# A hybrid encoder layer on one core: gates moved into a three-stage seven-product tail, divisions and roots on GpSimd, and every engine's order written by a list scheduler

## The chip, the core and the metric

The kernel runs on one core of one Trainium2 chip. The metric is device time in microseconds, the median of several executions. The engines are called TensorE (PE; PEld are its weight loads), VectorE (DVE), ScalarE (ACT), GpSimd (POOL) and SyncE (SP, whose queue issues the DMAs).

## What is computed

One layer, applied to two requests of 2048 tokens with 1024 features each, all in float32:

```python
h = rms_norm(x, norm_w)
q_a, k_a, v_a, g_a, q_b, k_b, v_b, g_b = split(h @ w_in)      # 512 128 128 512 512 512 512 512 columns
o_a = windowed_gqa_sink(rope(rms(q_a)), rope(rms(k_a)), v_a, sink) * silu(g_a)   # 8 heads, 2 key heads, +-128 tokens
o_b = neighbourhood_attn(rms(q_b), rms(k_b), v_b, rpb) * silu(g_b)               # 8 heads, 64-wide grid, window 8 x 16
x = x + concat(o_a, o_b) @ w_out
y = x + (p @ w_ple) * sigmoid(x @ w_ple_gate)
```

Both softmaxes are full ones (maximum, exponential, sum, division); group A has one more term, the sink, in its sum.

## The kernel before, in words

**Precision.** A float32 operand is split into a high part (`fp32r`) and the rest, and a product is made of three matmuls: high-high, high-low, low-high. So each 128-row step of a projection is three matmuls, and a 1024-row projection is 24 of them. A split is a ScalarE copy (high) and a subtraction (low) on VectorE or GpSimd.

**Stages.** Tokens go in tiles of 128, 16 a request. Group A has 32 tiles (`f` below 32), group B 64: two halves of four heads, each 32 tiles (8 rows x 16 columns of the grid).

- *Projections* are made by generators. `proj_a(f)` makes `pk` (keys and values, 256 columns, 24 matmuls), `pq` (queries, 512 columns, 24) and `pg` (gate A, 512 columns, 24). `proj_b(f)` makes `pqk` (512 columns) and `pvg` (values and gate, 512 columns). After the matmuls come the squares, `rsqrt` (a bit trick and three Newton steps, 11 small VectorE instructions), the normalisation, for A the rotation on GpSimd, for the gates `tanh` and one VectorE product into `gs`.
- *Attention* is made of units: `unit_a(f, kv)`, two a tile, and `unit_b(f)`, one a tile, four heads each. `sc` makes scores; `softmax` adds mask or bias and takes the maximum (VectorE, L204); `exps` does the exponential (L219) and reciprocal, and multiplies reciprocal and gate on GpSimd into `g` (L229). The probabilities are not divided. `pt` transposes them through TensorE and splits them, `po` multiplies by values, `fin` transposes the gate `g` (`pgt`, `pgtb`), multiplies it with the output (L539, L697) and stores it to `oa_d` or `ob_d` in HBM. `prep_a`/`prep_b` transpose queries and `split_q` splits them; L240 is the ScalarE copy that shifts a high half to the other 64 partitions.
- *Tail.* 16 output tiles of 256 tokens. Four are made directly (`out_ahead`, `pout`, 192 matmuls of 256 columns each) while the last units run. The other twelve go through six groups of 512 tokens in which a 2 x 2 block product is made of seven block products instead of eight (`STEPS`, `prep`, `product`, `result`); then eight such groups make the second stage, the sigmoid gate of the embedding. A block product is 48 matmuls of 256 columns (L973). `prep` makes sums of blocks (L939 to L950) and splits them; `result` adds the pieces. In the second stage `ple_of` makes the embedding product (`pple`) between the block products. The sums of weight blocks are made by GpSimd during group B (`combine`) and kept in `sums`. Between the two stages each weight quarter is replaced as soon as the last group has used it.

**Order.** `mm` and `tr` pin TensorE's order to program order (`pinned`). Units are interleaved with projections by hand: `PLAN_A` and `PLAN_B` say at which share of a unit's time each part is issued, and `stream` yields projection matmuls with their costs (215 for 512 columns) in between. Other engines follow the order in which the program names their instructions. All loads and stores are issued by SP, in order.

**Buffers.** PSUM: three banks for projections, three for scores and transposes, two for the rest (`PSB`). Five score buffers `s` in SBUF (`SB`), three `p_t`, five for V windows.

Of the kernel before, what the change touches and what calls it, by code (L numbers as in the profile page):

```python
# [46 lines left out]
def bias_offsets():  # L47
# [25 lines left out]
PLAN_A = (
# [3 lines left out]
)  # L77
PLAN_B = (
    (0.00, 1, "sc", 0), (0.03, 1, "sc", 1), (0.07, 1, "sc", 2), (0.09, 0, "po", 2), (0.11, 1, "sc", 3), (0.16, 0, "po", 3),
    (0.24, 0, "fin", 0), (0.35, 1, "prep", 0),  # L80
    (0.45, 1, "pt", 0), (0.52, 1, "pt", 1), (0.60, 1, "pt", 2), (0.66, 1, "po", 0), (0.74, 1, "pt", 3), (0.80, 1, "po", 1),
)


def emit(ctx, tc, io):
# [3 lines left out]
    pp = ctx.enter_context(tc.tile_pool(name="psum", bufs=2, space=bass.MemoryType.PSUM))  # L89

    def ptile(shape, tag, name):
        tag = PSM.get(tag, tag)
        return pp.tile(shape, F32, tag=tag, name=name, bufs=PSB[tag])

    ident = cp.tile([128, 128], F32, tag="ident", name="ident")
    make_identity(nc, ident)
    nw = cp.tile([128, KT], F32, tag="nw", name="nw")
    nc.sync.dma_start(nw, io["norm_w"])
    ms_a = cp.tile([128, 2 * NT], F32, tag="ms_a", name="ms_a")
    rs_b = cp.tile([128, 2 * NT], F32, tag="rs_b", name="rs_b")  # L100
    hr_b = cp.tile([128, 2 * NT], F32, tag="hr_b", name="hr_b")
    ep_b = cp.tile([128, 2 * NT], F32, tag="ep_b", name="ep_b")
    ms_b = cp.tile([128, 2 * NT], F32, tag="ms_b", name="ms_b")
    wk = cp.tile([128, 2], F32, tag="wk", name="wk")
    wkt = cp.tile([128, 4], F32, tag="wkt", name="wkt")
    nc.sync.dma_start(wkt, io["qk_norms"])
    nc.vector.tensor_tensor(out=wk[:, 0:1], in0=wkt[:, 0:1], in1=wkt[:, 1:2], op=ALU.mult)
    nc.vector.tensor_tensor(out=wk[:, 1:2], in0=wkt[:, 2:3], in1=wkt[:, 3:4], op=ALU.mult)
    nc.vector.tensor_scalar_mul(wk, wk, 0.125)
    nc.vector.memset(wk[0:16, 0:1], 0.125)  # L110
    nc.vector.memset(wk[64:80, 0:1], 0.125)
# [5 lines left out]

    def rsqrt(pool, v, y, n, tag):
        i2 = pool.tile([128, n], I32, tag=tag + "i", name=tag + "i")
        a = pool.tile([128, n], F32, tag=tag + "a", name=tag + "a")  # L120
        nc.vector.tensor_scalar(out=i2, in0=v.bitcast(I32), scalar1=1, scalar2=None,
                                op0=ALU.logical_shift_right)
        nc.vector.tensor_scalar(out=y.bitcast(I32), in0=i2, scalar1=-1, scalar2=0x5F3759DF,
                                op0=ALU.mult, op1=ALU.add)
        for _ in range(3):
            nc.vector.scalar_tensor_tensor(out=a, in0=y, scalar=-0.5, in1=y, op0=ALU.mult, op1=ALU.mult)
            nc.vector.tensor_tensor(out=a, in0=a, in1=v, op=ALU.mult)
            nc.vector.scalar_tensor_tensor(out=y, in0=a, scalar=1.5, in1=y, op0=ALU.add, op1=ALU.mult)

    copies = []  # L130

    def copied(src, rows, width):

        n = src.shape[1]
        d = dram.tile([rows, n], F32, tag=src.tensor.name + "_c", name=src.tensor.name + "_c")
        copies.extend((d[128 * j:128 * j + 128, c:c + width], src[128 * j:128 * j + 128, c:c + width])
                      for c in range(0, n, width) for j in range(rows // 128))
        return d

    def split_w(w, raw, sc):  # L140
        if sc is not None:
            nc.scalar.activation(w[:, 0], raw, AF.Copy, scale=sc)  # L142
            nc.vector.scalar_tensor_tensor(out=w[:, 1], in0=raw, scalar=sc, in1=w[:, 0].bitcast(F32),  # L143
                                           op0=ALU.mult, op1=ALU.subtract)
        else:
            nc.scalar.copy(w[:, 0], raw)
            nc.vector.tensor_tensor(out=w[:, 1], in0=raw, in1=w[:, 0].bitcast(F32), op=ALU.subtract)  # L147

    jobs = []

    def pump(n=1):
        for _, job in jobs[:n]:
            job()
        del jobs[:n]

    def flush(key):
        pump(max((i + 1 for i, (k, _) in enumerate(jobs) if k == key), default=0))

    def load_w(pool, tag, src, c0, nk, scaled):

        ws = []
        for j in range(nk):
            w = pool.tile([128, 2, 512], F32R, tag=f"{tag}{j}", name=f"{tag}{j}", bufs=1)
            raw = w[:, 1].bitcast(F32)
            nc.sync.dma_start(raw, src[128 * j:128 * j + 128, c0:c0 + 512])
            jobs.append((tag, partial(split_w, w, raw, nw[:, j:j + 1] if scaled else None)))
            ws.append(w)
        return ws

    def load_first(j0, w, src):  # L170

        n = w[0].shape[-1]
        st = main.tile([128, 2, 512], F32, tag="p_t", name="ws", bufs=3)
        nc.sync.dma_start(st[:, :, :n], src.rearrange("(j p) c -> p j c", p=128))
        for i in range(2):
            split_w(w[i], st[:, i, :n], nw[:, j0 + i:j0 + i + 1])
# [17 lines left out]
    def project(ps, xr, w, cost):  # L194

        for k in range(KT):
            for i, (a, b) in enumerate(((0, 0), (0, 1), (1, 0))):
                mm(ps, xr[:, a, k, :], w(k, b), k == 0 and i == 0, k == KT - 1 and i == 2)
                yield cost, k == KT - 1 and i == 2

    def softmax(i, ps, n, bias, sm):

        s = main.tile([128, 512], F32, tag="s", name="s", bufs=SB)
        nc.vector.tensor_tensor_reduce(out=s[:, :n], in0=ps[:, :n], in1=bias, scale=1.0, scalar=-3.0e38,  # L204
                                       op0=ALU.add, op1=ALU.max, accum_out=sm["mx"][:, i:i + 1])
# [944 lines left out]
```

## Time and profile before

| | |
|---|---|
| median of three executions | 2653.81 us (2651.65 to 2654.2) |
| span of the profiled execution | 2651.7 us, 2.1 below that median, at the low end of the three |
| TensorE busy | 2570.5 us, 97% |
| VectorE, ScalarE, GpSimd busy | 74%, 57%, 27% |
| granted TensorE clock, mean | 0.990 |
| HBM read and written | 266.33 and 105.92 MB |
| stages in the profiled execution | group A projections from 7.1 to about 775 us, group B from 775, direct output tiles and last units to about 1990, seven-product groups to 2646 |

How to read it: busy times of the engines overlap, so only the engine on which the others wait sets the time. A matmul's own duration in a row (about 400 ns at 512 columns, 283 at 256) is its way through a pipeline; the distance from one start to the next is what a stream of them costs. Busy time of a group in the list of lines counts only the union of its instructions.

### The profile page before, as it was taken

To read this page: it belongs to the slowest core of one execution; us is meant where nothing else is said; L and a number is where in the kernel's file an instruction comes from. 1 tells how busy PE (TensorE), PEld (TensorE's weight loads), DVE (VectorE), ACT (ScalarE), POOL (GpSimd) and SP (SyncE) were. 2 spreads that over 40 slices of the span, in tenths; PEclk is the share of its full clock that TensorE was granted. 3 is DMA by queue.
4 is the path that set the end of the run, shared out by engine and by line. 5 is a ranking of instruction groups with operands and counts; after the bars stand their busy time and mean duration, and the time that the engine had idled before them with its cause. 6 is when DMAs were issued, how large, how long until landed. Compare 5 with 4: busy or idle time off the path is not lost. (4 is left out here: it accounts for less than half of the span.)

```text
span 2651.7 us, 46657 instructions
## 1 busy us (share of the span) xinstructions
PE 2570.5 (97%) x16080; PEld 2270.6 (86%) x16080; DVE 1952.0 (74%) x5702; ACT 1500.2 (57%) x3519; POOL 703.2 (27%) x804
## 2 busy tenths in 40 slices
PE   7999999999989999999899999999989999999999
PEld 6888878888877888888788888888989999999999
DVE  6888878888887788788888888788665548555554
ACT  5776667676765566666676666666532214222322
POOL 3222222222222223223223222221123323223321
PEclk9999999999999999999999999999999999999999
DMA  6333322111233455555655554446675445223221
GB/s 208 101 100 102 108 74 77 58 55 52 55 98 117 150 170 171 181 177 160 221 167 165 185 170 153 148 152 205 184 235 195 158 158 194 79 97 107 80 76 48
DMA packets 230973, 357.48 MB, mean 135 GB/s; under 512 B 38321, under 2 KB 115761, under 8 KB 225585
## 3 DMA queue, kind: packets, MB, share of 16 engines
q1 hardware_dynamic: 230736, 354.51, 42.4%
q8 instruction: 127, 2.08, 0.3%
q14 instruction: 110, 0.89, 0.1%
HBM read 266.33 MB, written 105.92 MB: 140 GB/s over the span
## 5 line engine op out<-in xcount | busy, mean ns | idle before, releaser
L219 ACT ACTIVATE s<-s,nm 128x384 f32<-128x384 f32 (+4 forms) x512 | 306.3, 600 | 274.9 <-DVE nm L215 183.7
L189 PE MATMUL pvg<-wb,xr 128*128 128x512 f32 x1536 | 457.4, 405 | 0.0
L189 PE MATMUL pqk<-wa,xr 128*128 128x512 f32 x1536 | 436.6, 407 | 0.0
L279 POOL TENSOR_TENSOR xr<-stx,xr 128x512 fp32r<-128x512 f32 x192 | 246.9, 1296 | 396.1 <-ACT xr L278 369.2
L189 PEld LDWEIGHTS pqk<-wa,xr 128*128 128x128 f32 x1536 | 267.1, 189 | 36.8
L189 PEld LDWEIGHTS pvg<-wb,xr 128*128 128x128 f32 x1536 | 269.1, 190 | 31.8
L189 PE MATMUL pg<-wb,xr 128*128 128x512 f32 x768 | 231.9, 409 | 1.3 <-ACT wb L142 0.9
L189 PE MATMUL pq<-wa,xr 128*128 128x512 f32 x768 | 223.0, 404 | 3.5 <-DVE wa L143 2.3
L973 PE MATMUL acca<-opd,s 128*128 128x256 f32 x1344 | 169.6, 289 | 15.2 <-DVE r L992 13.6
L973 PEld LDWEIGHTS acca<-opd,s 128*128 128x128 f32 x1344 | 167.7, 197 | 15.8 <-DVE r L992 10.0
L189 PEld LDWEIGHTS pq<-wa,xr 128*128 128x128 f32 x768 | 141.6, 191 | 27.3 <-DVE wa L143 2.6
L204 DVE CUSTOM_DVE_ANT_0 s<-scb,bias 128x288 f32<-128x288 f32 (+3 forms) x256 | 141.9, 555 | 30.3 <-PE scb L189 26.4
L229 POOL TENSOR_TENSOR g<-qg,rd 128x256 f32<-128x256 f32 x64 | 39.2, 613 | 453.4 <-DVE rd L227 385.8
L668 DVE TENSOR_TENSOR p_t<-ptb,p_t 96x384 fp32r<-96x384 f32 (+3 forms) x256 | 149.6, 586 | 12.6 <-ACT p_t L667 9.1
L189 PEld LDWEIGHTS pob<-p_t,vw 128*128 128x128 f32 (+2 forms) x832 | 130.7, 190 | 32.4 <-ACT q1b L240 15.5
L189 PEld LDWEIGHTS pg<-wb,xr 128*128 128x128 f32 x768 | 137.2, 189 | 22.5 <-DVE wb L143 1.4
L667 ACT CAST p_t<-ptb 96x384 fp32r<-96x384 f32 (+3 forms) x256 | 129.8, 509 | 46.8 <-PE ptb L192 44.8
L556 DVE SCALAR_TENSOR_TENSOR ks_b<-pktb,wk,ks_b 64x128 fp32r<-64x128 f32 x256 | 115.2, 450 | 53.9 <-ACT ks_b L555 47.3
L189 PE MATMUL pob<-p_t,vw 128*128 128x256 f32 (+2 forms) x832 | 143.2, 285 | 5.4 <-ACT q1b L240 5.4
L189 PE MATMUL sc<-ks_a,q 128*128 128x384 f32 (+1 forms) x512 | 133.0, 351 | 13.2 <-DVE mx L204 6.4
L555 ACT ACTIVATE ks_b<-pktb,wk 64x128 fp32r<-64x128 f32 x256 | 124.9, 489 | 20.2 <-DVE ks_b L556 12.2
L204 DVE CUSTOM_DVE_ANT_0 s<-sc,mask 128x384 f32<-128x384 f32 (+1 forms) x256 | 136.0, 533 | 0.2
(197 smaller groups left out, 5826.3 us busy)
## 6 DMA issues: line engine op xcount, KB each, us to landing
stx<-x_b SPq DMA_DIRECT2D x128, 256.0 KB
vw<-v_d SPq DMA_DIRECT2D x112, 256.0 KB
stx<-x_a SPq DMA_DIRECT2D x64, 256.0 KB
stn<-x_n SPq DMA_DIRECT2D x64, 256.0 KB
v_d<-vb SPq DMA_DIRECT2D x64, 256.0 KB
x1r<-x_d SPq DMA_DIRECT2D x16, 1024.0 KB
y_t<-r SPq DMA_DIRECT2D x64, 256.0 KB
v_d<-vb SPq DMA_DIRECT2D x96, 128.0 KB
```

The costliest lines, as they stand in the source:

```text
L189: pinned(nc.tensor.matmul(out, lhsT, rhs, start=start, stop=stop))
L204: nc.vector.tensor_tensor_reduce(out=s[:, :n], in0=ps[:, :n], in1=bias, scale=1.0, scalar=-3.0e38, op0=ALU.add, op1=ALU.max, accum_out=sm[ ...
L219: nc.scalar.activation(ss[i][:, :n], ss[i][:, :n], AF.Exp, bias=nm[:, i:i + 1], accum_out=den[:, i:i + 1])
L229: nc.gpsimd.tensor_tensor(out=g2, in0=gs.rearrange("p (h d) -> p h d", h=4), in1=rd.unsqueeze(2).broadcast_to([128, 4, HD]), op=ALU.mult)
L279: nc.gpsimd.tensor_tensor(out=lo, in0=raw, in1=hi.bitcast(F32), op=ALU.subtract)
L555: nc.scalar.activation(hi, pkt[a:a + 64, i], AF.Copy, scale=wk[a:a + 64, 1:2])
L556: nc.vector.scalar_tensor_tensor(out=lo, in0=pkt[a:a + 64, i], scalar=wk[a:a + 64, 1:2], in1=hi.bitcast(F32), op0=ALU.mult, op1=ALU.subtract)
L667: nc.scalar.copy(p_t[:kc, :nch, 0], pf)
L668: nc.vector.tensor_tensor(out=p_t[:kc, :nch, 1], in0=pf, in1=p_t[:kc, :nch, 0].bitcast(F32), op=ALU.subtract)
L973: pinned(nc.tensor.matmul(ps[:, kk], w[k][:, a, c:c + 128], o[:, b, k], start=i in (0, 1, 4) and kk == 0 and k == 0 and j == 0, stop=k == ...
```

## The change

1. *Gates.* `pg` and the gate half of `pvg` are no longer projected per tile. The gates' weights (scaled by `norm_w` on GpSimd, stored to `w_g_c`) get their block sums in `combine`, now three pairs of matrices (twelve blocks instead of eight), and the tail gets a first stage: eight seven-product groups that make the gates from raw `x` (`x_r`). Its `result` multiplies by half the token's root (`hr_d`, broadcast over partitions), takes `tanh`, makes the SiLU on VectorE, multiplies on GpSimd with the attention output (a side load from `oa_d`/`ob_d`) and stores `og_d`. So `fin`, `g` and the transposes `pgt`/`pgtb` are gone, and the attention output is stored undivided by a gate.
2. *Tail.* All 16 output tiles go through seven-product groups (eight instead of six; `out_ahead` is gone). The tail has 24 groups in three stages, with two changes of weights. The last stage adds `x1` on GpSimd where VectorE did (L1006). The embedding products are made ahead (`embed`, 384 matmuls of 512 columns), stored halved in `ple_d`, and loaded by the last stage.
3. *Softmax.* Each head's probabilities are divided on GpSimd before the transposes, four instructions a unit.
4. *Roots* are one GpSimd instruction each (`pow` with exponent -0.5) instead of 11 on VectorE.
5. *Shifted query halves* come from a DMA inside SBUF instead of ScalarE.
6. *Order.* Every instruction or small bundle becomes an `Op` with an engine, a planned duration, dependencies, a priority and the buffer slots it takes and frees. `Flow.run` plays them while the program is built: at each moment each free engine takes the ripe op of the best priority, and the op's instructions are emitted then. `Ordered` keeps that order on all engines. Attention outranks projections (`low`), which outrank embedding products in group B. All eight PSUM banks are one pool; there are nine score buffers. A projection op is three matmuls.

The core of the diff (moved code and unchanged arithmetic left out):

```diff
+    def emit(self, o, t):
+        dur, tail = o.dur if isinstance(o.dur, tuple) else (o.dur, self.TAIL[o.eng])
+        if o.eng == "SP":
+            self.wire = max(t + 700, self.wire) + tail
+            o.end = (self.wire, self.wire + 1250)
+            self.clock["SP"] = max(t + dur, self.wire - AHEAD)
+        else:
+            o.end = (t + dur, t + dur + tail)
+            self.clock[o.eng] = t + dur
...
+    def rsqrt(v, y, n, deps, prio):
+        return op("POOL", 250 + 175 * n, lambda: G.tensor_tensor(out=y, in0=v, in1=half_neg[:, :n], op=ALU.pow), deps, prio)
...
-        pg = ptile([128, 512], "pj", "pg")
-        for i, c in enumerate(project(pg, xr, lambda k, b: w_g[k][:, b, :], 215)):
...
-        gs = ap.tile([128, 512], F32, tag="qg", name="gs", bufs=6)
-        nc.scalar.activation(gs, pg, AF.Tanh, scale=y[:, 11:12])
-        nc.vector.scalar_tensor_tensor(out=gs, in0=gs, scalar=1.0, in1=pg, op0=ALU.add, op1=ALU.mult)
...
+            o3 = dma(lambda e=e, z=z: hi[e]()[z:z + 64].bitcast(F32), lambda e=e, a=a: hi[e]()[a:a + 64].bitcast(F32), w / 4, [o1], pr)
...
+        r = op("DVE", 100, lambda: V.reciprocal(out=rd, in_=den), ex, pr)
+        dv = [op("POOL", 100 + 1.45 * n, lambda i=i: G.tensor_scalar(
+            out=ss[i].t[:, :n], in0=ss[i].t[:, :n], scalar1=rd[:, i:i + 1], scalar2=1.0, op0=ALU.mult, op1=ALU.mult),
+            [r], pr + 0.01 * i) for i in range(4)]
...
-        pv = ptile([128, 512], "pj", "pvg")
+        vb, vops = project(f, "pv", 256, 120, xs, xdone, w_v, v_done, low(prios[1]), free=[xs])
...
+    LA, LB = 2, 7
+    for f in range(2 * NT):
+        proj_a(f, w_k, wx_done, w_q, wq_done, set_ops)
+        if f % NT == NT - 1:
+            regroup(f // NT)
+        if f >= LA:
+            q = prep_q(f - LA)
+            for kv in range(2):
+                unit_a(f - LA, kv, q)
...
+    groups = [(stage, g) for stage in range(3) for g in range(NU)]
...
+            z = op("DVE", 612, lambda: V.tensor_tensor(out=v3(rt.t), in0=v3(src()),
+                                                       in1=rs.t[:, TW * t:TW * t + TW].unsqueeze(1).broadcast_to([128, 2, TW]), op=ALU.mult),
+                   [pe, r[1], rl], pr, take=[rt] if single else (), free=[rs, *(free if single else ())])
+            a = op("ACT", 540, lambda: A.activation(th.t, rt.t, AF.Tanh), [z], pr, take=[th])
+            y = op("DVE", 612, lambda: V.scalar_tensor_tensor(out=rt.t, in0=th.t, scalar=1.0, in1=rt.t, op0=ALU.add, op1=ALU.mult),
+                   [a], pr, free=[th])
...
+                    G.tensor_tensor(out=rt.t, in0=rt.t, in1=sd(), op=ALU.mult)
...
+            if g == NU - 1 and stage < 2:
+                load_q(stage + 1, STEPS[i], T0 + 7 * n + i + 1, product_ops[7 * n + i])
```

In group B the units run seven tiles behind the projections (`LB`), in group A two (`LA`). `wa`/`wb` hold query-key weights and are reloaded between the halves of B and for the tail, as before.

More of the change, by code (lines that the diff above doesn't have):

```diff
@@ L1 @@
+import heapq
+from bisect import insort
 from contextlib import ExitStack
 from functools import partial
-from itertools import chain, islice
 import numpy as np
@@ new lines, with __init__, when @@
+class Pool:
+    def __init__(self, tiles, in_turn=False):
+        self.tiles, self.in_turn, self.shared = list(tiles), in_turn, False
+        self.made, self.given = 0, 0
+        self.idle = [(0.0, i) for i in range(len(self.tiles))]
+class Slot:
+    def __init__(self, pool, keep=0):
+        self.pool, self.i, self.t, self.left, self.at, self.keep = pool, None, None, 0, 0.0, keep
+        self.turn = pool.made
+        self.readers = {}
+        pool.made += 1
+    def when(self):
+        p = self.pool
+        if len(p.idle) <= self.keep or p.in_turn and self.turn != p.given:
+            return float("inf")
+        return sorted(p.idle)[self.keep][0]
@@ L130, in emit @@
[L130 to L168, printed above, removed]
@@ new lines, in emit, with more_operands @@
+    sum_pool = pool(2, [128, 4, TW], F32, "sum", cx, True)
+    th_pool = pool(2, [128, 512], F32, "th", cx)
+    root_pool = pool(2, [128, 512], F32, "root", cx)
+    od_pool = x_pool
+    ple_end = [o for b in range(NU) for o in ple_ops[b]]
+    def more_operands():
+        od_pool.tiles.append(mid.tile([128, 2, KT, 128], F32R, tag="raw", name="opd", bufs=1))
+        od_pool.idle.append((F.t, 2))
+    op("NOP", 0, more_operands, ple_end)
+    groups = [(stage, g) for stage in range(3) for g in range(NU)]
@@ new lines, in emit, with product, go @@
+    acc, part, roots = {}, {}, {}
+    def product(m):
+        n, i = divmod(m, 7)
+        stage, g = groups[n]
+        od, o4, hi, lo = operand(m)
+        w, wd = w_tiles[STEPS[i]], w_done[stage, STEPS[i]]
+        key = "c" if i in (1, 4, 5) else "a"
+        new = i in (0, 1, 4)
+        product_ops[m] = []
+        for mp in range(2):
+            if new:
+                acc[key, mp] = [Slot(banks), None, None]
+            st = acc[key, mp]
+            prev = st[1]
+            for kk in range(2):
+                def go(kk=kk, st=st, mp=mp):
+                    ps, o = st[0].t[:, 256 * kk:256 * kk + 256], o4()
@@ new lines, in emit @@
+    load_q(0, "s4", T0 + 3, ple_end)
+    for n, (stage, g) in enumerate(groups):
+        load_raw(n)
+        if stage == 0:
+            rs = Slot(root_pool)
+            roots[g] = (rs, dma(lambda rs=rs: rs.t, hr_d[512 * g:512 * g + 512].partition_broadcast(128), 256, (), T0 + 7 * n - 5, take=[rs]))
+        for i in range(7):
+            product(7 * n + i)
+            if g == NU - 1 and stage < 2:
+                load_q(stage + 1, STEPS[i], T0 + 7 * n + i + 1, product_ops[7 * n + i])
+    F.run()
```

1636 lines of the change are left out of this document (827 added, 809 removed), and 3 rows, old and new, of the table PLAN_A.

## Prediction

> **What bounds the kernel now.** I read the page's busy times first, then the cores view for the granted clock.
>
> ```profile
> PE 2570.5 (97%) x16080; PEld 2270.6 (86%) x16080; DVE 1952.0 (74%) x5702; ACT 1500.2 (57%) x3519; POOL 703.2 (27%) x804
> core 0: 2651.7 us, clock 0.990
> ```
>
> TensorE is the bound. It is idle for 2651.7 - 2570.5 = 81.2 us, and the clock it is refused costs 1% of 2651.7 = 26.5 us: 107.7 us of stall. All else is matmul issue, so I count matmuls, at start-to-start spacings, not the pipelined 400 ns that a group row gives as mean. The timeline of group B and the chain give these:
>
> ```profile
> 1201.32 1.17 PE L189 MATMUL pqk<-wa,xr 128*128 128x512 f32 x4
> 1202.33 0.49 PE L192 MATMUL ptb<-ident,s 128*96 128x128 f32 x3
> 1202.57 0.94 PE L189 MATMUL pqk<-wa,xr 128*128 128x512 f32 x3
> 1206.01 2.23 PE L189 MATMUL pqk<-wa,xr 128*128 128x512 f32 x9
> 1208.08 0.32 PE L189 MATMUL scb<-ks_b,q1b 128*128 128x360 f32 x1
> 2004.16 11.52 PE accc L973 x96
> ```
>
> Nine 512-column matmuls start 1208.08 - 1206.01 = 2.07 us apart: 0.230 each. Ninety-six of 256 columns take 11.52: 0.120 each. From 1201.32 to 1202.57 pass 1.25 us for four matmuls (0.92) and three transposes: 0.11 each. A seven-product group is 7 x 48 matmuls of 256 columns: 336 x 0.120 = 40.3 us. Then windows over steady stretches and over the places with gaps:
>
> ```profile
> 130.70:323.60 192.90, 190.86 (x1066) 160.84 (x1065) 159.93 (x609) 135.74 (x353) 49.10 (x97) 1.00 0.31 99
> 923.30:1184.80 261.50, 260.05 (x1411) 217.16 (x1409) 211.88 (x657) 178.35 (x433) 76.21 (x76) 1.00 0.55 173
> 0.00:10.00 10.00, 2.58 (x8) 1.90 (x9) 2.54 (x9) 4.68 (x9) 4.69 (x11) 1.00 0.67 211
> 10.00:20.00 10.00, 8.60 (x45) 8.05 (x46) 6.32 (x20) 7.77 (x20) 2.96 (x3) 0.83 0.95 300
> 20.00:30.00 10.00, 6.45 (x20) 4.66 (x19) 8.03 (x39) 4.76 (x12) 3.21 (x8) 0.78 0.99 316
> 780.00:800.00 20.00, 14.27 (x53) 11.01 (x54) 16.13 (x46) 13.41 (x32) 4.18 (x4) 0.83 0.11 34
> 1840.00:1860.00 20.00, 17.90 (x119) 17.01 (x119) 15.80 (x35) 12.18 (x28) 0.74 (x1) 0.83 0.72 216
> 1980.00:2000.00 20.00, 10.25 (x65) 10.05 (x64) 16.30 (x17) 2.10 (x2) 12.21 (x9) 0.74 0.65 207
> 2200.00:2220.00 20.00, 16.16 (x113) 16.01 (x112) 20.00 (x27) 10.03 (x17) 5.49 (x2) 0.83 0.79 263
> 2640.00:2652.00 12.00, 6.54 (x55) 6.33 (x53) 3.47 (x6) 1.19 (x2) 0.00 (x0) 0.93 0.19 66
> ```
>
> Idle plus clock lost: start 12.4 + 3.9 = 16; end 5.5 + 0.8 = 6; A to B (780) 5.7 + 3.4 = 9; last tiles (1840) 2.1 + 3.4 = 5.5; tail's start (1980) 9.8 + 5.2 = 15; change of weights between the tail's two stages (2200) 3.8 + 3.4 = 7. That is 59; the other 48 is scattered. The tail's steady groups lose nothing.
>
> **The change, part by part.** The list scheduler runs while the program is built; what reaches the chip is an order of each engine's queue. First TensorE's own work, with the groups' counts:
>
> ```profile
> L189 PE MATMUL pvg<-wb,xr 128*128 128x512 f32 x1536 | 457.4, 405 | 0.0
> L189 PE MATMUL pg<-wb,xr 128*128 128x512 f32 x768 | 231.9, 409 | 1.3 <-ACT wb L142 0.9 <-DVE wb L143 0.4
> L189 PE MATMUL pple<-p_r,wp 128*128 128x256 f32 x768 | 102.6, 283 | 0.0
> L189 PE MATMUL pout<-o_r,wa 128*128 128x256 f32 x384 | 58.7, 294 | 3.4 <-DVE o_r L743 2.7 <-ACT o_r L742 0.7
> L192 PE MATMUL pgt<-ident,g 128*128 128x128 f32 x128 | 24.3, 272 | 0.0
> L192 PE MATMUL pgtb<-ident,g 128*128 128x128 f32 x128 | 24.3, 271 | 1.5 <-DVE rqba L127 1.5
> ```
>
> Gate A leaves: 768 x 0.230 = -176.6. `pvg` halves to `pv`: 1536 x 0.110 = -169.0. Gate transposes leave: 256 x 0.11 = -28.2. Four direct output tiles (`pout`, twice x384) leave: 768 x 0.120 = -92.2, and become two groups: +80.6. Eight gate groups come: +322.6. Embedding, 768 at 256 columns to 384 at 512: 88.3 - 92.2 = -3.9. Sum: **-66.7 us**.
>
> This counts only if other engines keep up with shorter tiles. The first steady window holds eight A tiles (x8 below), 24.1 us each; the new one is 24.1 - 24 x 0.230 - 4 x 0.11 = 18.1. The second holds sixteen B tiles (384 `pqk` matmuls, 24 a tile), 16.3 each; new 16.3 - 24 x 0.110 - 2 x 0.11 = 13.5.
>
> ```profile
> L189 PE MATMUL pqk<-wa,xr 128*128 128x512 f32 x384 | 109.7, 407 | 0.0
> L126 DVE SCALAR_TENSOR_TENSOR rqaa<-y 128x8 f32<-128x8 f32 x24 | 4.0, 168 | 0.5
> L440 DVE SCALAR_TENSOR_TENSOR gs<-gs,pg 128x512 f32<-128x512 f32 x8 | 5.4, 670 | 0.0
> L539 DVE TENSOR_TENSOR ot<-pgt,ot 128x256 f32<-128x256 f32 x16 | 6.8, 424 | 1.1
> L227 DVE TENSOR_SCALAR rd<-rd,y 128x4 f32<-128x4 f32 x16 | 3.4, 212 | 0.0
> L439 ACT ACTIVATE gs<-pg,y 128x512 f32<-128x512 f32 x8 | 5.5, 683 | 0.0
> L240 ACT CAST q<-pqt 64x512 fp32r<-64x512 f32 x16 | 9.3, 581 | 0.4
> L229 POOL TENSOR_TENSOR g<-gs,rd 128x256 f32<-128x256 f32 x16 | 9.8, 613 | 16.8 <-DVE rd L227 16.8
> L279 POOL TENSOR_TENSOR xr<-stx,xr 128x512 fp32r<-128x512 f32 x16 | 20.6, 1285 | 28.1 <-ACT xr L278 28.1
> ```
>
> VectorE, A tile: 159.9/8 = 20.0; the roots (22 small instructions a tile like L126, 0.168 each, 3.7) and L440, L539, L227 (15.6/8 = 1.95) go: 14.4 of 18.1. ScalarE: 135.7/8 = 17.0 less (5.5 + 9.3)/8: 15.1 of 18.1. In B, VectorE needed 211.9/16 = 13.2 and ScalarE 11.1 with nothing removed; both are under 13.5.
>
> GpSimd, A tile: 49.1/8 - 9.8/8 = 4.9 stays. Eight divisions of 384 columns: no row has this form; above, L229 scaled, 613 x 384/256 = 0.92 each; below, VectorE's rate in L440, 670 x 384/512 = 0.50. I take 0.92, the row of the same engine: 7.4. `pow` has no row: between nothing and what the Newton chain took, 1.8 each; I take the middle, 1.8 for the two. Sum 14.1 (8.9 to 15.9) of 18.1. In B: 76.2/16 less one L229, plus four divisions and one root, 9 of 13.5; the weight sums, twelve blocks instead of eight, add under 1. Not the bound, so nothing is charged. The longer chain (divisions between reciprocal and transposes, 4 x 0.92 = 3.7 us a unit) is covered by nine score buffers instead of five and by projections; uncovered in all 64 A units it would cost 237.
>
> Query halves are now shifted by two DMAs per tile instead of L240. The chain shows a 128 KB DMA at 3.81 us against 0.58:
>
> ```profile
> 1945.57 3.81 DMA ob_d<-o_tb
> SPq L261 <- POOL xr L279: 527.7, 169, 12.5
> PE acca L973 <- DVE r L992: 13.6, 2, 9.8
> ```
>
> The 192 DMAs stand in SP's one queue, whose head waits for others up to 12.5 us (second line); behind them wait loads of x, V windows and bias. They are issued about one tile (13 to 18 us) before use: nothing charged, rival below. The gate stage also adds side loads and `og_d` round trips: per 40.3 us two 1 MB loads, eight 256 KB loads, eight stores, about 6.3 MB or 156 GB/s, under the 316 GB/s of the third window.
>
> The tail. Here GpSimd and VectorE meet. Timeline, then line L1006, whose VectorE input pair lies in SBUF:
>
> ```profile
> 2402.99 2.41 POOL L939 TENSOR_TENSOR opd<-sum,opd 128x1024 fp32r<-128x1024 f32 x1 [8.83 <-ACT opd L925]
> 2404.19 1.75 DVE L1006 SCALAR_TENSOR_TENSOR r<-r,x1r 128x512 f32<-128x512 f32 x1
> L1006 DVE SCALAR_TENSOR_TENSOR r<-r,x1r x64: 683/692/2870, 2247.1 to 2647.9; 128x512 f32<-128x512 f32 x64
> L939 DVE TENSOR_TENSOR opd<-x1r,opd 128x1024 fp32r<-128x1024 f32 x9 | 11.0, 1226 | 15.4 <-ACT opd L925 15.4
> ```
>
> The VectorE instruction, 0.69 alone, starts under a GpSimd one and ends 0.55 after it: it stood still meanwhile. So I add both. Gate group: GpSimd five passes of 2.4 and eight products of 1.29 (L279's size), 22.3; VectorE with two SBUF inputs nine of 1.23 and fourteen of 0.69 (six scalings by the roots, eight SiLU products), 20.7. Together 43.0, against 40.3 of TensorE. As 0.14 of each instruction did overlap (23 x 0.14 = 3.2), the excess is between -0.5, so 0, and 2.7 a group: 0 to 22 us over eight. I take 12. Third stage: 22.3 + 9 x 1.23 + 8 x 0.69 = 38.9, under 40.3: nothing. The second has 12 + 11: nothing. [...]
>
> Stalls. Start 16 and end 6 stay (gate A's 2 MB of weights leave the start, which may save the 3.6 us that PE idles from 20 to 30: kept in the range). A to B stays, 9. The change of weights (third line of the queue fence: PE waits there too) happens twice, 14. The tail's start and last tiles (20.5) go: 88 us of embedding products are the lowest-priority filler there; were these used up, the 20.5 return. Of the scattered 48 I keep half, lacking a row that says which; ends 0 and 48. That makes 69 against 107.7: **-39**.
>
> Total: 2651.7 - 66.7 - 39 + 12 = 2558; the median of runs is 2.1 above the profiled span: **2560**.
>
> **Rivals.**
> (1) Everything scattered and A to B is filled too, ports free: 2560 - 24 - 9 - 12 = 2515, about 2500 with both changes of weights hidden. For it: steady windows are 99% busy. Against: durations in a plan are not those of a run.
> (2) The old stalls come back elsewhere: 2560 + 39 = 2599, 2606 with the second change of weights on top.
> (3) Ports fully serial: VectorE's evictions (six additions and two scalings from PSUM, 8 x 0.69 = 5.5) queue behind blocked instructions too. Gate group 43.0 + 5.5 = 48.5, +8.2; third stage 38.9 + 6 x 0.69 = 43.0, +2.7; eight each, 87 in place of 12: 2635. For it: L1006's 2870 ns. Against: its median of 692 says that most were not blocked.
> (4) Slower: PE's queue now waits in each tile for the shifted query halves behind SP's queue. Scores outrank projections, so in an in-order queue no projection fills that wait. It decides from (2654 - 2560)/96 = 0.98 us a tile on; one 3.81 us DMA exposed in every second tile gives 96 x 1.9 = 183, so 2743. For it: the 12.5 us queue heads. Against: the steady windows show 1.5 to 2 us of PE idle in whole stretches, though SP waited there as much. [...]
>
> **How the numbers follow.** Forecast 0.60 (2520 to 2598); rival 1 0.10; rival 2 0.09; rival 3 0.08; no change 0.04; rival 4 0.09. A measurement of this kernel tells 0.2% (5 us) from no change. Faster 0.87, same 0.04, slower 0.09. The range runs from rival 1's 2500 to rival 3's 2635 and leaves out 4 and "no change".
>
> **What would show it.** Right: 256-column projections `pv` at 0.120, no `pgt`, tail groups 40 to 43 us, two gaps at changes of weights, GpSimd near 60 to 80% in A. Wrong: PE waits on query tiles or SP in every tile; GpSimd over 18 us a tile (slow `pow` or division); gate groups near 48 us.

## The result, and the profile after

The changed kernel takes **2729.3 us** (median of four executions) against 2652.7 of the kernel before on the same chip: ratio 1.029 (95% interval 1.0273 to 1.0307), slower. The prediction was 2560, range 2500 to 2635. One of the four ran at a granted clock of 0.71, took 3253.2 us and is left out of the ratio; the other three took 2726.8, 2727.3 and 2731.3, so a difference from 2729.3 given below may be 2 us too large. The profiled execution has a span of 2729.5 us. From its page: engines, clock, packets.

```profile
PE 2567.4 (94%) x17264; PEld 2313.6 (85%) x17264; DVE 1949.8 (71%) x4054; ACT 1549.6 (57%) x3449; POOL 1462.6 (54%) x1517
core 0: 2729.5 us, clock 0.983
DMA packets 319466, 472.01 MB, mean 173 GB/s; under 512 B 72784, under 2 KB 178384, under 8 KB 309712
```

TensorE's busy time, 2570.5 before, has hardly changed, though 67 us of matmul issue went: a matmul of 512 columns counts as busy for 0.39 us, though the next can start 0.23 us after it, so short waits hide in the figure. Idle time grew from 81 to 162 us. By stages, the windows view (group A, eight tiles; group B; a steady group of the gate stage; one of the out stage). The last two rows have the first and last start of group B's projections, 512 columns (`wb`) and 256 columns (`wa`). (Rows of after name the helper that keeps the order, L210, or a matmul helper, whatever made the instruction.)

```profile
130.00:274.80 144.80, 144.05 (x844) 121.94 (x843) 125.61 (x393) 119.84 (x328) 96.06 (x162) 1.00 0.41 122
720.00:1500.00 780.00, 735.29 (x4420) 620.72 (x4419) 547.86 (x1393) 536.50 (x1250) 427.94 (x458) 0.99 0.67 208
1841.80:1884.05 42.25, 40.78 (x338) 40.38 (x338) 34.69 (x32) 14.86 (x21) 27.98 (x17) 1.00 0.50 157
2109.60:2149.85 40.25, 40.25 (x338) 40.25 (x337) 20.26 (x23) 7.34 (x7) 12.02 (x5) 1.00 0.60 207
L268 PE MATMUL bank<-wb,xr x1536: 387/393/776, 592.6 to 1543.8; 128*128 128x512 f32 x192
L268 PE MATMUL bank<-wa,xr x1536: 274/283/583, 614.5 to 1558.3; 128*128 128x256 f32 x192
```

Group A is as predicted, 18.1 us a tile with TensorE full, away from its two regroupings. Group B's projections take 1558.3 - 592.6 = 966 us, 15.1 a tile, where 64 x 13.5 = 864 were predicted. No engine is near full there: TensorE 94%, VectorE 70%, ScalarE 69%, GpSimd 55%. The tail's 24 groups take 1029 us from first to last start, where 24 x 40.3 are 967: the first two gate groups 55.7 and 48.9, the steady ones 42.3, the two at each change of weights 48.7 + 50.1 and 44.5 + 45.5. So 102 us are lost in B (11 of them in one gap at its start, shown below) and 62 in the tail (26 of those predicted: ports 12, changes of weights 14).

Part of this stands in the scheduler's own plan. Played through by itself, `Flow.run` of the changed kernel ends at 2606 us, 46 over the forecast, and has B's projections at 911 us, 47 over the 864. So the chip adds 55 us in B to what the plan already has; what makes the plan itself that long was not tested.

**Where B's queues stand.** The timeline of a tile's key instructions, ScalarE's high halves and VectorE's low halves, after (first two rows) and before (the others); then the waits view, VectorE, from 720 to 1500 us, after and before (total, times, longest).

```profile
737.71 2.00 ACT L210 ACTIVATE big<-bank,wk 64x128 fp32r<-64x128 f32 x4 [1.31 <-PE bank L271]
739.74 1.85 DVE L210 SCALAR_TENSOR_TENSOR big<-bank,wk,big 64x128 fp32r<-64x128 f32 x4 [2.47 <-ACT big L210]
1203.33 0.48 ACT L555 ACTIVATE ks_b<-pktb,wk 64x128 fp32r<-64x128 f32 x1
1205.09 0.49 ACT L555 ACTIVATE ks_b<-pktb,wk 64x128 fp32r<-64x128 f32 x1
1203.92 0.46 DVE L556 SCALAR_TENSOR_TENSOR ks_b<-pktb,wk,ks_b 64x128 fp32r<-64x128 f32 x1
1205.61 0.45 DVE L556 SCALAR_TENSOR_TENSOR ks_b<-pktb,wk,ks_b 64x128 fp32r<-64x128 f32 x1 [0.32 <-ACT ks_b L555]
DVE big L210 <- ACT big L210: 85.4, 47, 2.8
DVE ks_b L556 <- ACT ks_b L555: 32.9, 68, 0.7
```

Before, the hand-written order put other work between the four. The scheduler puts four on ScalarE in a row, and VectorE's first, which needs only the first of them (done at about 738.2), starts when the fourth has ended (739.71). It stands at the head of VectorE's queue meanwhile. The scheduler knows of no such wait; it plans the four 0.40 us apart, and they start 0.50 apart.

The trace's semaphore records show where the wait comes from. After, in 56 of 58 groups of four, only VectorE's first instruction waits for the semaphore that ScalarE raises, and the other three wait for nothing of ScalarE's; so that one wait has to cover all four results. Before, each of the last three waits for itself, in all 60 groups. Accordingly VectorE's first starts after the end of ScalarE's fourth in 56 of 57 groups after, and in none of 58 before. So the wait lies in the signals of the built program, in which the four stand in a row, and not in a delay of the chip.

**Where the loads stand.** At the first regrouping (tile 16), DMA issues, TensorE's next gap, and three windows; last the waits of ScalarE and TensorE at the second, 585 to 620 us.

```profile
284.55 0.43 SPq L210 DMA_DIRECT2D ms_d<-ms_a  x1
285.06 2.35 SPq L210 DMA_DIRECT2D hr_d<-hr_a  x1
299.91 6.03 SPq L210 DMA_DIRECT2D ms_b<-ms_d  x6
306.16 2.08 PE L268 MATMUL bank<-wa,xr 128*128 128x512 f32 x4 [8.48 <-DVE mx L210]
280.00:290.00 10.00, 10.00 (x58) 8.05 (x56) 7.93 (x24) 9.50 (x27) 8.60 (x15) 1.00 0.57 111
290.00:300.00 10.00, 7.24 (x45) 6.17 (x44) 3.84 (x11) 1.13 (x2) 3.25 (x6) 1.00 0.41 15
300.00:310.00 10.00, 3.84 (x9) 3.10 (x10) 4.60 (x19) 5.11 (x16) 0.35 (x1) 0.52 0.27 48
ACT wa L210 <- DMA wa<-w_in_c: 10.8, 1, 10.8
PE bank L271 <- POOL raw L210: 11.1, 1, 11.1
```

`hr_d` is new: 2048 elements of 4 bytes, one transfer, planned as 37 ns of transfer time. From 290 to 300 us the DMA engines are 41% busy and move 15 GB/s; the next loads of x come late, and TensorE stands 8.5 us (clock 0.52 in the next window). `ms_d` and `ms_b` move single elements too, but they were there before, when TensorE's longest wait at this place was 5.3 us.

### The profile page after: what moved, and what is told of

Its sections match the earlier page's. It is cut to its first block, busy times and chain, and to the rows that moved or that the text cites. A ratio compares the mean times of both kernels' runs of the same rounds, so it can differ in the third digit from the quotient of the medians.

```text
span 2729.5 us, 49655 instructions
## 1 busy us (share of the span) xinstructions
PE 2567.4 (94%) x17264; PEld 2313.6 (85%) x17264; DVE 1949.8 (71%) x4054; ACT 1549.6 (57%) x3449; POOL 1462.6 (54%) x1517
## 5 line engine op out<-in xcount | busy, mean ns | idle before, releaser
L268 PE MATMUL bank<-wa,xr 128*128 128x256 f32 (+1 forms) x2304 | 413.3, 326 | 14.2 <-DVE mx L210 11.4
L210 POOL TENSOR_SCALAR s<-s,rd 128x384 f32<-128x384 f32 (+4 forms) x512 | 291.1, 587 | 250.9 <-DVE rd L210 118.6
L268 PE MATMUL bank<-wb,xr 128*128 128x512 f32 x1536 | 405.4, 401 | 2.0 <-DVE big L210 1.6
L210 POOL TENSOR_TENSOR xr<-st,xr 128x512 fp32r<-128x512 f32 x208 | 268.2, 1291 | 216.9 <-ACT xr L210 200.1
L268 PEld LDWEIGHTS bank<-wa,xr 128*128 128x128 f32 x2304 | 337.9, 192 | 49.7 <-DVE mx L210 15.8
L210 ACT ACTIVATE s<-s,nm 128x384 f32<-128x384 f32 (+4 forms) x512 | 307.2, 602 | 81.3 <-DVE nm L210 79.3
L268 PEld LDWEIGHTS bank<-wb,xr 128*128 128x128 f32 x1536 | 274.8, 190 | 49.3 <-DVE big L210 1.8
L1066 PE MATMUL bank<-xr,s 128*128 128x256 f32 x2304 | 287.0, 285 | 15.2 <-DVE s L210 10.8
L1066 PEld LDWEIGHTS bank<-xr,s 128*128 128x128 f32 x2304 | 282.5, 194 | 17.0 <-issue 7.7
L210 DVE TENSOR_TENSOR p_t<-bank,p_t 128x512 fp32r<-128x512 f32 (+3 forms) x440 | 263.0, 624 | 41.5 <-ACT p_t L210 38.8
L268 PE MATMUL bank<-big,q 128*128 128x384 f32 (+4 forms) x1024 | 253.3, 355 | 22.3 <-DVE mx L210 8.4
L210 POOL TENSOR_TENSOR y<-vr,half_neg 128x8 f32<-128x8 f32 (+1 forms) x128 | 186.6, 1458 | 136.1 <-DVE vr L210 124.7
L210 ACT CAST p_t<-bank 128x512 fp32r<-128x512 f32 (+3 forms) x440 | 223.9, 541 | 53.5 <-PE bank L271 44.0
L210 DVE TENSOR_TENSOR s<-bank,s 128x512 f32<-128x512 f32 x208 | 142.5, 686 | 146.5 <-PE bank L1066 145.0
L210 DVE SCALAR_TENSOR_TENSOR big<-bank,wk,big 64x128 fp32r<-64x128 f32 x320 | 137.6, 430 | 110.2 <-ACT big L210 103.0
L210 DVE TENSOR_TENSOR ot<-bank,ot 64x256 f32<-64x256 f32 (+1 forms) x256 | 141.7, 553 | 85.9 <-ACT ot L210 81.4
L210 ACT COPY ot<-bank 64x256 f32<-64x256 f32 (+1 forms) x256 | 121.4, 474 | 125.5 <-PE bank L268 98.8
```

Source lines behind the costliest of these rows:

```text
L210: return lambda *a, **k: self.tc.keep_in_program_order(f(*a, **k))
L268: pinned(nc.tensor.matmul(out, lhsT, rhs, start=start, stop=stop))
L1066: pinned(nc.tensor.matmul(ps, w[k][:, x, c:c + 128], o[:, y, k], start=new and kk == 0 and k == 0 and j == 0, stop=k == 3 and j == 2, skip ...
```

## The experiments

Theories. **Head of queue:** the order is made for planned times, each engine keeps it, and whatever the plan does not know (a hidden wait, a slow transfer) makes the engines stand in turn. Rivals: **rate** (the plan's 4.65 ns per KB makes it think B is bound by transfers), **slack** (0.3 us too little for TensorE), **shift** (the prediction's rival 4), **long chain** (GpSimd's divisions), **ports** (GpSimd against VectorE in the gate stage). The times of B below are those of its projections, 966 us in the changed kernel.

**The scheduler's constants.**

```diff
-                  deps, prio, take, free, tail=4.65 * kb)
+                  deps, prio, take, free, tail=3.3 * kb)      # e1
-MARGIN = {"NOP": 0, "PE": 300, ...
+MARGIN = {"NOP": 0, "PE": 1500, ...                           # e2
-            o.end = (self.wire, self.wire + 1250)
+            o.end = (self.wire, self.wire + 2500)             # e8
```

> One constant of the scheduler is changed: a transfer is planned at 3.3 ns per KB instead of 4.65. In the kernel's plan group B then no longer has its transfers busy all the time, so projections are put earlier and attention is spread. If the planned transfer rate is what costs group B its 75 us (theory rate): B projections take 890 to 930 us instead of 966, the time 2660 to 2700. If the cause is that matmuls are placed without slack for late inputs (theory slack), or the shifted query halves behind SP's queue (theory shift): B stays at 950 to 980 and the time at 2715 to 2740. If the lower rate makes loads come late everywhere: over 2745.

> One constant is changed: the scheduler lets TensorE use what another engine made 1500 ns after its planned end instead of 300 ns. Theory slack (TensorE's in-order queue waits at each small delay because the plan leaves 0.3 us): the 137 us that TensorE loses in the window from 720 to 1520 us halve, B takes 890 to 920 us, the time is 2650 to 2680. Theory rate: B stays near 960, the time 2715 to 2735. Theory shift: the shifted halves get no more slack from their own queue than 1.2 us, so at most half of the gain: 2690 to 2720.

> One constant is changed: the scheduler takes a transfer as landed 2.5 us after its bytes have passed instead of 1.25. If late loads at the head of ScalarE's, VectorE's and GpSimd's queues (11 us at 293, 11 at 597, 16 at 1684, 8 at 2018) are planned too early by a constant latency: those shrink, the time is 2695 to 2715. If they come from a few slow or delayed transfers: no gain, and a longer pipeline for the shifted query halves costs some: 2730 to 2760.

Measured: e1 2747.8 (ratio 1.036 to before), B 983. e2 2717.4 (1.025), B 971 and group A 9 us shorter. e8 2734.4 (1.031). Against 2729.3, only slack gains, 12 us, and not in B. None of the three is the cause of B's loss.

**Shift and division undone.** In e3 `prep_q` copies the halves on ScalarE (`A.copy` for `dma`). In e7 `dv` is the exponentials' own ops: the division is left out, and the output is not normalised.

> The two halves of each query tile are moved to the other partitions by ScalarE copies instead of 192 transfers (the part of the change that rival 4 blames is undone). Theory shift: the waits in group A and B go, the time is 2620 to 2680. Theories rate and slack: ScalarE has 96 x 2 copies of about 0.4 us more and 30% to spare, the chain is shorter by a transfer but no matmul gets slack: 2720 to 2745.

> The softmax divisions (512 GpSimd instructions) are left out, so attention is not normalised: each chain from scores to transposes is shorter by 0.5 to 0.7 us and one engine. Theory long chain (GpSimd in the attention chain costs group B its 75 us): B takes 890 to 930 us, the time is 2650 to 2690. Theory head of queue: the same waits stand elsewhere, B takes 940 to 970, the time is 2700 to 2730.

Measured: e3 2771.8 (1.045): 43 slower, group A 36 of it. So the transfers that rival 4 blamed cost less than ScalarE copies in their place; that they cost nothing e3 does not show, but over the whole trace of the changed kernel only 1.7 us of TensorE's waits end with one of them. e7 2726.1 (1.028), B 968: without any division B is as long. GpSimd's division is not in the way.

**Element-wise transfers.** e4 spreads `hr_d`, one column after each tile. e5 removes them:

```diff
+            tr(kb.t[:16, :128], ms_a[:, c])
+            tr(kb.t[:16, 128:256], hr_a[:, c])        # 16 rows of 512 B, then to ms_d and hr_d
-        ls = [dma(ms_b[:, i:i + 1], ...) for i in range(NT * s, NT * s + NT)]
+        ls = [dma(mx_t[4 * b:4 * b + 4] ..., ...) for b in range(4)]   # runs of 64 B, turned by TensorE
```

> The halved roots for the gates go to DRAM in 32 transfers of 128 elements, one after each A tile, instead of two transfers of 2048 elements at the regroupings. If those two transfers are what holds up the loads of x at 285 and 590 us (TensorE's gaps of 8.5 and 11.1 us): both gaps shrink and the time falls by 10 to 20, to 2710 to 2720. If the 16 transfers for ms_b, or the order around them, are the cause: within 4 us of the changed kernel, 2725 to 2733.

> The mean squares and halved roots are turned by TensorE at the two regroupings (three transposes each) and go to DRAM and back in rows of 64 B and more; the transfers of single 4-byte elements (36 with 8192 elements in all) are gone. If element-wise transfers hold up the queue (32 more of them cost 93 us in group A, 2.9 each): TensorE's gaps of 8.5 us at 298 and 11 us at 600 go, group A ends 10 to 20 us earlier, the time is 2700 to 2715. If those gaps come from the order around them alone: 2722 to 2733.

Measured: e4 2823.7 (1.066). I had expected a gain of 10 to 20; it lost 94, nearly all in group A, whose end came 93.7 us later: 93.7/32 = 2.9 us for each transfer of 512 bytes in 128 elements. e4 moves as many elements and bytes as the changed kernel, only in 32 transfers instead of 2, so this is the price of a transfer where it stands in the queue, not of its elements. SP's queue stood 25 us for the roots in e4 (15 waits between 40 and 560 us); what the rest is was not separated. From 285 to 325 us the trace of the changed kernel has 6576 packets under 512 bytes, where `ms_d`, `hr_d` and the 16 `ms_b` have 6144 elements: about one packet for each element. e5, with runs of 64 bytes and more, takes 2708.7 (1.022, interval 1.0198 to 1.0232): 20.6 less, 15 in group A. The windows of e5 at the same place:

```profile
290.00:300.00 10.00, 9.79 (x57) 8.55 (x58) 9.47 (x36) 7.43 (x23) 4.95 (x9) 1.00 0.38 107
300.00:310.00 10.00, 8.02 (x49) 6.70 (x47) 8.21 (x27) 6.61 (x17) 8.96 (x13) 1.00 0.15 46
```

TensorE is busy 9.8 and 8.0 of 10 us where it was 7.2 and 3.8.

**The hidden waits of the keys.** e6 tells the scheduler; e9 also alternates the two key tiles:

```diff
-                o2 = op("DVE", 375, k2, [o1], pr, free=[kb])
+        keys_of[f] = his + [op("DVE", 375, k2, his, pr, free=[kb]) for k2 in los]     # e6: all four
-        for i in range(2):
-            for e in range(2):
+        for e in range(2):
+            for i in range(2):                                                        # e9
```

> In group B the trace shows VectorE's first key instruction of a tile starting only when the last of the tile's four ScalarE key instructions has ended (0.5 to 1.5 us later than the one whose result it reads; 63 us in the window from 720 to 1520), which the scheduler does not know. Here it is told so: each of the four VectorE instructions depends on all four of ScalarE. Theory head of queue (an instruction that stands at the head of an in-order queue for something that the plan put earlier): VectorE does other work meanwhile, group B's projections take 890 to 930 us instead of 966, the time is 2670 to 2695. If VectorE's standing is hidden and group B is short of something else: 950 to 970 and 2715 to 2730.

> As the run in which the scheduler knows that VectorE's key instructions wait for all four of ScalarE, and the four are put in the order tile 0, tile 1, tile 0, tile 1 instead of 0, 0, 1, 1. The trace shows instructions that write the same key tile one after the other starting 0.50 us apart although the scheduler has them at 0.40. If the spacing is a wait between neighbours on one tile, it goes to 0.40, and 8 x 0.1 us a tile on the two engines come free: B's projections take 925 to 945 us instead of 955, the time is 2690 to 2708. If it is a wait on any earlier one: no change, 2710 to 2719.

Measured: e6 2714.5 (1.024), B 955: 15 less. B lies in the rival's range and the time just under it, so knowing of this wait alone gives back 11 of B's 102 us. e9 2694.9 (1.016, 1.0141 to 1.018), B 932: 34 less. The timeline of a tile's keys in e9, its waits in the same window, and the last start of B's projections:

```profile
734.30 1.49 ACT L210 ACTIVATE big<-bank,wk 64x128 fp32r<-64x128 f32 x4 [1.31 <-PE bank L271]
735.82 1.61 DVE L210 SCALAR_TENSOR_TENSOR big<-bank,wk,big 64x128 fp32r<-64x128 f32 x4 [1.96 <-ACT big L210]
DVE big L210 <- ACT big L210: 56.5, 43, 2.2
L268 PE MATMUL bank<-wa,xr x1536: 274/283/415, 613.1 to 1522.7; 128*128 128x256 f32 x192
```

Four now take 1.49 instead of 2.00 us on ScalarE and 1.61 instead of 1.85 on VectorE. But not for the reason that I expected. Within the fours of group B (medians of 56 to 61), starts are apart, in us:

| | first to second | second to third | third to fourth |
|---|---|---|---|
| ScalarE, after | 0.50 | 0.50 | 0.50 |
| ScalarE, e9 | 0.28 | 0.47 | 0.29 |
| VectorE, after | 0.46 | 0.47 | 0.46 |
| VectorE, e9 | 0.36 | 0.45 | 0.36 |

In e9 every step goes to the other tile, and still the middle one is slow. What changes only there is `e`, the half of the partitions (0 to 63 or 64 to 127) that is read and written, and with it the place in the row of the key tile; in the old order it changed at every step. So the longer spacing goes with this change, and not with the tile: 0.50 against 0.28 on ScalarE, 0.46 against 0.36 on VectorE. Where it is long, in the changed kernel, an instruction starts 13 ns (ScalarE) or 15 ns (VectorE) after the end of the one before it (medians), which takes 0.49 or 0.45 us; in e9 one takes 0.48 or 0.45, so where `e` stays the next starts before that end. That it is the partitions rather than the place in the row, no run separates. In e9 VectorE's first still waits for ScalarE's fourth (one wait in all 61 groups), but the fourth ends 0.5 us earlier and the plan knows.

**Ports.** In e10 `gate()` runs on VectorE (`V.tensor_tensor`, planned 680 ns) instead of GpSimd.

> The gate product (eight instructions a gate group) runs on VectorE instead of GpSimd. Theory ports (GpSimd's and VectorE's two-input instructions exclude each other, and their sum sets the gate group): the sum falls by 8 x (1.29 - 0.69) = 4.8 us from 43.0 to 38.2, under TensorE's 40.3, so steady gate groups go from 42.3 to 40.3 to 40.8 us and the time falls by 10 to 16, to 2712 to 2720. If the 2 us a group come from something else (a load, a chain): groups stay at 42 to 43, or VectorE becomes the bound and they go to 44.

Measured: 2715.9 (1.024), 13 less, in the expected range, but not by the expected way: steady groups go from 42.3 to 42.1 only. The gain lies in the first three groups (147.4 to 143.8 together), the first change of weights (48.7 + 50.1 to 44.4 + 46.3) and an earlier start of the tail (3). What a steady group loses is seen in the timeline, after (five rows) and e10 (two):

```profile
1855.61 2.79 POOL L210 TENSOR_TENSOR opd<-sum,opd 128x1024 fp32r<-128x1024 f32 x1 [1.16 <-ACT opd L210]
1856.66 2.83 DVE L210 TENSOR_TENSOR sum<-sum,raw 128x1024 f32<-128x1024 f32 x1
1860.79 0.63 ACT L210 ACTIVATE th<-s 128x512 f32<-128x512 f32 x1 [3.45 <-DVE s L210]
1862.26 1.07 ACT L210 COPY s<-bank 128x512 f32<-128x512 f32 x2
1862.89 1.33 PE L1066 MATMUL bank<-xr,s 128*128 128x256 f32 x9 [0.82 <-ACT s L210]
1935.33 2.89 DVE L210 SCALAR_TENSOR_TENSOR s<-th,s 128x512 f32<-128x512 f32 x1
1941.02 1.22 PE L1066 MATMUL bank<-xr,s 128*128 128x256 f32 x8 [1.56 <-ACT s L210]
```

A VectorE pass planned at 1.15 us takes 2.83 under a GpSimd one; the `tanh` stands 3.45 us at the head of ScalarE's queue for VectorE; the copy behind it is what frees TensorE's partial sum. In e10 another VectorE instruction (0.68 alone) is stretched to 2.89, and TensorE waits 1.56 at the same copy. So the two engines do contend, but their sum does not set the group. That the price comes through the order of the queues is a reading of these rows; no run shows it, and e17, which plans such passes longer, leaves the steady groups at 42.1.

**Changes of weights, and all together.** e11 lets ScalarE's splits of new weights go one product (5.8 us) later; e12 has e5, e9, e10 and e11.

> At the two changes of weights, ScalarE's split of a step's new weights is let go one product (5.8 us) later than the load's start. Theory head of queue (ScalarE stands 8 us at 2018 for a load that the plan had landed, and the casts behind it make TensorE wait): the groups around the two changes, 48.7 + 50.1 and 44.5 + 45.5, fall to 41 to 44 each, the time by 10 to 20, to 2707 to 2718. If the load itself is what TensorE waits for: unchanged or longer, 2725 to 2735.

> Four edits together: regrouping through TensorE, known key waits with alternating tiles, gate product on VectorE, late split. If the causes are separate, their gains add: 20 + 15 to 30 + 10 to 16 + 10 to 20 less than 2729, 2645 to 2675, about the kernel before. If they share cover (TensorE's queue waits for the next late thing): 2680 to 2705.

Measured: e11 2727.2 (1.028): within 2 us, no gain. e12 2665.5 (1.005, 1.0035 to 1.0068): 64 less than the changed kernel; the single gains add to 20.6 + 34.4 + 13.4 + 2.1 = 70.5 (against 2727.3 they add to 62.5, and e12 gains 62). So the causes are nearly separate.

**What is left.** With e5, e9 and e10: e13 has the rate at 4.0; e14 has 3.8 and durations from the traces (for instance `k1` 398 to 290); e15 leaves out the low halves of group B's probabilities; e16 is e14 with splits three products later; e17 also plans VectorE's 1024-column passes at 1.6 us; e18 does that alone on e14.

> Regrouping through TensorE, known key waits with alternating tiles, gate product on VectorE (as e12_all without the late split), and a planned transfer rate of 4.0 ns per KB instead of 4.65. The kernel's own plan ends 30 us earlier with it (2570 instead of 2601). Theory rate: the gain shows now that the hidden waits are gone, the time is 2630 to 2650, under the kernel before. If the chip's loads are then late at the head of queues as in e1: 2665 to 2690.

> As e13 with 3.8 ns per KB, and the scheduler's durations set to what the traces show: key instructions 0.29 and 0.365 us instead of 0.40 and 0.375, copies of two on one tile 0.1 longer, GpSimd's divisions shorter (0.55 instead of 0.66 at 384 columns), the maximum's sign change 0.18 instead of 0.09. Theory durations (the order is made for other times than the chip's): the difference between the time and the plan's end, 72 us in e12 and 123 in the changed kernel, falls under 60, the time is 2620 to 2640. If an in-order queue loses to small delays whatever the mean durations: difference 70 or more, 2640 to 2670.

> As e12_all without the late split; in group B the low halves of the transposed softmax (256 VectorE instructions of 0.45 to 0.69 us, 2.1 us a tile) are left out, so the products use stale low halves. Theory VectorE (its in-order queue is what TensorE waits for in group B): projections take 880 to 905 us instead of 940. If TensorE's order alone costs it: 930 to 945. The drain after group B is not compared.

> As e14, and at the changes of weights ScalarE's splits of a step are let go three products (17 us) after the load may start, where e11 had one. Theory head of queue: ScalarE no longer stands for a load, the groups around the changes (50.4, 46.6 and 44.3, 42.1) fall to 40.5 to 44, the time by 8 to 18, to 2637 to 2647, under the kernel before. Theory bandwidth (TensorE waits for the weights or other loads themselves): the sum of the four groups stays within 4 us, the time 2650 to 2658.

> As e16, and the scheduler takes VectorE's passes of 1024 columns in the tail at 1.6 us instead of 1.15 (the trace shows 1.22 alone and 2.4 to 2.9 beside GpSimd). Theory order (TensorE's 1 to 2 us wait a gate group for ScalarE's copy comes from a plan that has VectorE too fast): gate groups go from 42.1 to 40.5 to 41.5, another 5 to 12 less than e16. If the stretch is where it is whatever the order: 42 to 43, the time within 5 of e16 or above.

> As e14, with VectorE's passes of 1024 columns in the tail planned at 1.6 us instead of 1.15 and nothing else. If e17's 9 us over e16 come from that, it holds here too: 2643 to 2649, under the kernel before by 0.1 to 0.3%. If they were the luck of one order: 2651 to 2660.

Measured: e13 2656.1 (1.0007, 0.9998 to 1.0017), e14 2654.6 (1.0003, 0.9993 to 1.0012), e16 2658.3 (1.0025, 1.0015 to 1.0035), e17 2649.5 (0.9995, 0.9986 to 1.0005), e18 2649.1 (0.9997, 0.9989 to 1.0006). The rate, worse alone, gains about 10 over e12 once the waits are mended (e12's late split alone was worth 2). e14's time is 83 us over its plan's end (2571.5), where e12's is 65 over its own (2601; the 72 of the expectation is a slip), so the theory that durations alone would bring the two together falls. In e16 ScalarE no longer stands for weights, but the four groups at the changes take 186.6 us against 183.4 in e14: TensorE's wait has moved to an addition on VectorE. ScalarE's wait after (first row), TensorE's after (second) and in e16 (third), then what VectorE does meanwhile in e16, and the window of that wait:

```profile
2026.26 0.62 ACT L210 CAST wb<-wb 128x512 fp32r<-128x512 f32 x1 [7.98 <-DMA wb<-w_out_c]
2084.52 1.84 PE L1066 MATMUL bank<-xr,s 128*128 128x256 f32 x7 [7.55 <-DVE s L210]
1995.85 1.41 PE L1079 MATMUL bank<-xr,s 128*128 128x256 f32 x5 [6.25 <-DVE s L210]
1986.06 6.29 DVE L210 TENSOR_TENSOR s<-s 128x512 fp32r<-128x512 f32 x4
1985.45:1995.63 10.18, 4.15 (x35) 3.94 (x33) 10.18 (x9) 5.15 (x9) 7.87 (x3) 0.93 0.56 162
```

VectorE waits for no load there: it is busy for all of the 10.18 us, with low halves of new weights ahead of the addition, four in 6.29 us where one alone takes 0.67, while GpSimd is busy for 7.87. So the expectation's rival, the loads, gets the sum right, but the trace points to VectorE's queue; no run took that work away. In e17 gate groups stay at 42.1: the planned 1.6 does nothing there. e18 is 5 us under e14 (its groups around the second change of weights take 43.3 and 40.3 us instead of 44.3 and 42.1), with intervals that overlap. e15 took 2676.2 as a whole; its B is 914 us, against 940 in e12. Windows of e12 and e15, 720 to 1450 us (VectorE is the third busy time):

```profile
720.00:1450.00 730.00, 688.69 (x4185) 589.46 (x4183) 516.80 (x1328) 488.46 (x1180) 414.10 (x441) 0.98 0.69 215
720.00:1450.00 730.00, 702.31 (x4308) 605.64 (x4307) 430.58 (x1177) 501.07 (x1217) 408.05 (x438) 0.99 0.69 213
```

Taking a sixth of VectorE's work out gives back 26 us of B, a fifth of the 64 x 2.1 = 134 taken: VectorE's load is part of what is left, not all. No version is faster than the kernel before by what can be told; e13, e14, e17 and e18 are level with it.

## Why the prediction was wrong

- **TensorE's work, -66.7: right where it can be seen.** A tiles 18.1, out and third-stage groups 40.3, `pv` at 256 columns. A gate group was given as 40 to 43 and is 42.3.
- **GpSimd not the bound: right.** 96.06/8 = 12.0 us an A tile against 14.1 predicted (8.9 to 15.9). The division is nearer its lower bound, `pow` nearer the upper end:

```profile
L210 POOL TENSOR_SCALAR s<-s,rd 128x384 f32<-128x384 f32 x164 | 94.9, 596 | 85.6 <-ACT sq L210 52.8 <-DVE rd L210 12.7 <-ACT xr L210 6.6
L210 POOL TENSOR_TENSOR y<-vr,half_neg 128x8 f32<-128x8 f32 x23 | 37.8, 1646 | 14.1 <-DVE vr L210 13.9
L210 POOL TENSOR_TENSOR y<-vr,half_neg 128x3 f32<-128x3 f32 x23 | 19.8, 863 | 10.5 <-DVE vr L210 10.5
```

- **Ports, +12 in the gate stage: right in size** (8 x 2.0 = 16), by luck: in e10 the sum of the two engines fell by 4.8 us a group in the forecast's own count, below TensorE's 40.3, and the steady group only by 0.2. The choice of passes to count, VectorE's with both inputs in SBUF, is borne out in the changed kernel's gate stage (1694 to 2110 us): the 23 SiLU products `s<-th,s` that start under a GpSimd instruction take 0.70 to 2.93 us (median 1.22) against 0.68 otherwise, while the 20 passes that read PSUM (`s<-bank,s` and `s<-bank,root`) and start under one take 0.67 to 0.69.
- **The step that failed is the one for group B: "both are under 13.5", and nothing charged.** An engine's busy sum below TensorE's is a bound, not a price. B cost 102 us; the forecast had 9 of them, the gap between A and B, and the rest was priced at nothing, though 47 of the 102 stand in the scheduler's plan. Of the 102, e9 showed 34 to be the keys' waits and spacing (B 932); no full version came under e16's 926.5, so some 62 are left, of which VectorE's load is a part (e15) and the rest stays open. The reading that fits is that in-order queues which feed each other in a ring (TensorE, ScalarE, VectorE, TensorE) add up their waits when each tile's cover shrinks from 16.3 to 13.5 us; e6 and e9 support it for one wait, and no run shows it for the rest.
- **The stalls, -39: wrong in sign.** Idle time doubled. "Tail's start and last tiles (20.5) go" failed most plainly: the first two gate groups alone lose 24 us. "Two changes of weights, 14" were 28 (188.8 - 4 x 40.3).
- **A transfer was left out.** The change's `hr_d` write appears nowhere in the sum; with its neighbours `ms_d` and `ms_b`, which were there before, it cost 20.6 us (e5). The row that could have warned was in the trace before: the `ms_b` loads, 128 elements of 4 bytes each.
- **What the parts leave.** 102 in B and 62 - 26 = 36 in the tail make 138 of the 169 us missed. The rest lies in A's regrouping and in the stretch between B's last projection (1558) and the tail's first group (1694), and was not separated.
- **The rivals.** Rival 2, old stalls elsewhere, has the right mechanism, far too small (2599). Rival 4 named the right kind of place, an in-order queue standing in each tile of B, but the wrong culprit: e3 made it slower by 43. The clock falls beside short waits too: between 612 and 1543 us no gap of TensorE is longer than 1.55 us, and yet the granted clock halves five times (0.50 from 850 to 856 us, for instance), for 20 us in all.

## What to carry to other kernels

A static order is as good as its knowledge of waits: before trusting a schedule's busy sums, look in the trace for instructions that start later than the end of what they read, see in the semaphores which signal they wait for, and give the planner that wait or remove it. Read the plan's own end before forecasting: here it was 46 us over the forecast. Look at the shape and number of transfers as well as their bytes, and when an engine has fewer microseconds of filler per tile, charge each hop of the chain that the filler used to hide. Undo one part at a time: here undoing the parts suspected first (shift, division) gained nothing, and two edits, keys and regrouping, held 55 of 77 us.

## What the runs showed of the hardware that was not expected

- Transfers of 4-byte elements: 15 GB/s at a 41% busy share from 290 to 300 us, behind two of 2048 elements each. Spread out, each of 32 transfers of 128 elements cost 2.9 us of group A (e4), queue waits included.
- Between neighbours that change the partition half, starts are 0.2 us further apart on ScalarE and 0.1 on VectorE (64x128, 0.47 to 0.50 against 0.28 and 0.45 to 0.47 against 0.36, table above; the place in the row changes with it).
- The granted clock halved in B, for 20 us in all, with no TensorE gap over 1.55 us.
- GpSimd multiplies 128x384 by a scalar per row (the reciprocal) in 0.596 us, faster than the 0.66 that the plan had, and needs 1.646 us for eight roots a row, 0.863 for three.
- A VectorE pass of 1024 columns with both inputs in SBUF, 1.23 us alone, took 2.83 beside a GpSimd one; one of 512 columns took 2.89 instead of 0.68 (e10). The contention was forecast; that the sum of the two engines does not set the group's time was not.
